# New matmul durations in a planner: fp32r matmuls of 256 and 512 columns

## The chip, the cores and the metric

The kernel runs on one core of a Trainium2 chip, as one launch. The metric is the device time in microseconds (us), the median of several executions. A core has a matmul engine (TensorE; PE in the profile, PEld for its weight loads), three engines for elementwise work (VectorE is DVE, ScalarE is ACT, GpSimd is POOL) and a queue engine (SyncE, SP), which here issues most loads; POOL issues the loads that add to what is already in the buffer.

## The reference

Two layers over 512 rows of width 1024, all in fp32. Each layer is a feed-forward part, a token mixing part and a second feed-forward part, and an RMS norm closes the whole:

```python
for l in range(DEPTH):                                   # DEPTH = 2
    x = x + 0.5 * swiglu_ffn(rmsnorm(x, ffn1_norm[l]), ffn1_w_in[l], ffn1_w_out[l])
    h = rmsnorm(x, mix_norm[l])
    u_rwkv, u_gla, u_xa, u_gate = split_cols(h @ w_in[l], ...)
    y_rwkv, v_first = rwkv7_mixer(u_rwkv, v_first, ...)
    y_gla = gla_mixer(u_gla, ...)
    y_xa = memory_attention(u_xa, rmsnorm(mem, mem_norm[l]), xa_w_kv[l])
    branches = jnp.stack([y_rwkv, y_gla, y_xa], axis=2)
    gates = jax.nn.sigmoid(u_gate.reshape(b, s, N_BRANCH, d))
    x = x + jnp.einsum('bsjc,jcd,bsjd->bsd', branches, w_branch[l], gates) @ w_out[l]
    x = x + 0.5 * swiglu_ffn(rmsnorm(x, ffn2_norm[l]), ffn2_w_in[l], ffn2_w_out[l])
return rmsnorm(x, final_norm)

def swiglu_ffn(h, w_in, w_out):                          # w_in 1024 x 5632, w_out 2816 x 1024
    gate, up = jnp.split(h @ w_in, 2, axis=-1)
    return (jax.nn.silu(gate) * up) @ w_out
```

## The kernel before

**Matmuls.** Activations lie transposed in SBUF: 128 partitions of a width tile by 512 rows, and a half of the rows is 256 columns. A large product in near fp32 is made of fp32r matmuls: each operand is split into a high part (a copy in fp32r, made on ACT: `hi`, `hl`, `mh`, `whi`) and a low part (source minus high part, made on DVE: `lo`, `hl` again where one tile holds both, `ml`, `wlo`), and three matmuls give high by high, high by low and low by high. In the mixing part such products have 512 columns, beside many small matmuls, most of them in fp32. In the feed-forward parts nearly all are 256 columns wide.

**Feed-forward parts.** They run as a chain of jobs (`seven`, L931). A job is one 2 x 2 block product of weights and activations, done with seven half products in place of eight, from sums and differences of the blocks. Its weights come as `wraw`, `q`, `e` (named `q` in the profile) and `d`; the loads on POOL add a block to one that SP has loaded. DVE makes two more sums of weights, `q<-wraw` and `q<-q`, and ACT and DVE split each weight. The half products gather in three PSUM tiles: X is `ps_b`, Y is `ps_i`, Z is `ps_f` and `ps_c` in turn. ACT copies X into Y once, early in the job: the row `ps_i<-ps_b`. In the first phase of a block (from `w_in`) the evictions give `ft` and `fm`, and then `mh`, `ml` and `s` (operands for the second phase); in the second phase (from `w_out`, the down products) each PSUM tile is added to the residual on DVE: `x<-ps_i`, `x<-ps_c`, `x<-ps_f`, `x<-ps_b`. `chain` (L982) starts a job before the former is ended, so the next job's weight sums stand among the former's evictions.

**What sets the order.** Nothing is issued when the network's functions run. A `Recorder` notes every operation with its dependencies, and `cost` (L353) gives each a `busy` (how long it keeps its engine) and a `took` (until its result is there). `plan` then simulates the five engines. `run` takes on PE the ready matmul that is first in the program, small ones ahead of large products, and in the current mode if it can (`choose`); on the other engines it takes the ready operation with the smallest due time. Due times come from `urgency`: PE's order of the last simulation is added up by `busy`, and from there the time goes back through `took`. This is done six times, each with due times from the order before it, and the order with the earliest simulated end is kept. `issue` emits it, so that each engine's queue holds its instructions in this order. Hence all instructions have the line L318 in the profile, the line that emits.

Of the kernel before, what the change touches and what calls it, by code (L numbers as in the profile page):

```python
# [286 lines left out]
class Recorder:  # L287
# [65 lines left out]
    def cost(self, o, ins, outs, a, k):  # L353

        out = outs[0] if outs else None
        col = any(v.n == 1 and not v.flat for v in ins[1:])
        psum = any(v.psum for v in ins)
        if o.engine == "tensor":
            n = out.n
            wide = ins[0].n > 64  # L360
            if o.what == "transpose":
                o.busy, o.took = 109, 275
            elif ins[0].dt == F32R:
                o.busy = n / 2.4 + 13.7
                o.took = n / 2.4 + 177
            else:
                o.busy = 2 * max(108 if wide else 58, 2 * n / 2.4 + 2.7)
                if self.tiles > 1:
                    o.busy = 2 * max(108 if wide and n <= 64 else 54, 2 * n / 2.4 + 2.7)
                o.took = o.busy / 2 + 2 * n / 2.4 + 168  # L370
                o.busy = max(o.busy / self.tiles, 110 if wide else 56)
            up = lambda q: 32 if q <= 32 else 64 if q <= 64 else 128
            o.mode = (o.what != "transpose" and ins[0].dt == F32R, up(ins[0].rows[1] - ins[0].rows[0]), up(ins[0].n))
        elif o.engine == "vector":
            n = max(v.n for v in ins + outs)
            if o.what == "reciprocal":
                o.took = 130 + 6.3 * n
            elif o.what == "tensor_tensor_scan":
                o.took = 139 + 2.11 * n
            elif o.what == "memset":  # L380
                o.took = 60 + n / 0.96
            else:
                fast = o.what in ("tensor_scalar", "tensor_copy") and not psum
                o.took = ((n / 2 if fast else n) + 151) / 0.96 + (55 if col and o.what != "tensor_tensor" else 0)
            o.busy = max(o.took - 80, 60)
        elif o.engine == "scalar" and o.what != "dma_start":
            n = out.n
            o.took = 0.83 * n + (166 if psum else 207) + (90 if col else 0) + (95 if "accum_out" in k else 0)
            o.busy = o.took - 90 + (100 if "accum_out" in k else 0)
            o.table = {AF.Tanh: "exp", AF.Exp: "exp", AF.Sqrt: "sqrt", AF.Ln: "ln", AF.Silu: "silu",  # L390
                       AF.Sigmoid: "sig"}.get(a[2])
        elif o.engine == "gpsimd" and o.what == "dma_start":
            o.pipe = 4 * out.n * P / 190
            o.busy, o.took = 1000, o.pipe + 2950
        elif o.engine == "gpsimd":
            o.took = 95 + 0.84 * out.n
            o.busy = o.took
        else:
            some = ins + outs
            size = 4 * some[0].n * (1 if some[0].flat else some[0].rows[1] - some[0].rows[0])  # L400
            o.pipe = size / 230
            o.busy, o.took = 440 if o.engine == "scalar" else max(440, o.pipe), o.pipe + 1450
# [1539 lines left out]
```

## Time and profile before

| | |
|---|---|
| median of 3 executions | 2520.64 us (2519.31 to 2521.92) |
| the profiled execution | 2520.57 us, its span 2518.8 us |
| mean granted TensorE clock | 0.998 of full speed |
| instructions in the span | 47196, of them 17636 on PE |
| large stretches | first layer: FFN 1 to about 340 us, mixing to 885, FFN 2 to 1252; second layer: FFN 1 to 1585, mixing to 2130, FFN 2 and the closing norm to the end |

The profile is of one execution. Busy shares are those of the span; an engine's rows can overlap, since the next instruction starts before the last is through, so the step from one start to the next tells what an instruction costs in a row of them. In timeline rows stand the start, the duration, engine, line, operation, the tiles (out<-in), the shape and a count, and in brackets the engine's idle time ahead of it with what ended it.

### The profile page before, as it was taken

Reading aid. Unit: us, or ns where it says so; the run is one execution under the profiler, and the core shown is the slowest. Engines: PE = TensorE matmul, PEld = TensorE weight load, DVE = VectorE, ACT = ScalarE, POOL = GpSimd, SP = SyncE. Lnnn points to the kernel's source line nnn. Section 1 sums busy time; section 2 is a strip of 40 time slices with the busy share of each in tenths; the row PEclk is TensorE's granted clock in tenths of the full one; section 3 lists DMA queues with packets and bytes.
Section 4 is the critical chain, followed back from the end, with each engine's and each line's share of the span. In section 5 each row is a group of like instructions: output and inputs, shape, how many; then the busy total and the mean of one; then the engine's idle time right before and its main releaser. Section 6 shows DMA issues by size and latency. Waiting matters only on the chain.

```text
span 2518.8 us, 47196 instructions
## 1 busy us (share of the span) xinstructions
PE 2490.5 (99%) x17636; PEld 2241.0 (89%) x17636; DVE 2096.8 (83%) x4218; ACT 1468.8 (58%) x2660; POOL 241.3 (10%) x363
## 2 busy tenths in 40 slices
PE   9999999999999999999999999999999999999998
PEld 8999988888788899999989999877887888899998
DVE  8988886688888689988899889766879877898888
ACT  6665666564554456565665656674645434565655
POOL 1121100000000001211111111000000000011110
PEclk9999999999999999999999999999999999999999
DMA  7787762322222456877658787523322225468774
GB/s 196 200 203 191 173 188 74 117 75 70 75 77 74 144 159 152 209 192 185 158 138 190 190 189 185 162 90 93 90 67 84 68 78 172 134 164 197 190 185 107
DMA packets 163669, 358.02 MB, mean 142 GB/s; under 512 B 18257, under 2 KB 38161, under 8 KB 163441
## 3 DMA queue, kind: packets, MB, share of 16 engines
q1 hardware_dynamic: 125344, 288.87, 36.8%
q0 software_dynamic: 36864, 65.03, 16.6%
q8 instruction: 139, 2.28, 0.4%
q10 hardware_dynamic: 1232, 1.11, 0.1%
q14 instruction: 90, 0.73, 0.1%
HBM read 342.88 MB, written 12.06 MB: 141 GB/s over the span
## 4 chain that ended last, share of the span: by engine, by line
PE 85%; DVE 8%; DMA 3%; ACT 2%; issue 2%; POOL 0%; DVEq 0%; SPq 0%; ACTq 0%; POOLq 0%
PE ps_b L318 43%; PE ps_i L318 24%; PE ps_f L318 9%; PE ps_c L318 8%; PE ps_y L318 2%; DMA q<-in_ffn_out_dram 1%; DVE lo L318 1%; DVE hl L318 1%; DVE wlo L318 1%; DMA wraw<-in_ffn_in_dram 1%; DVE x L318 1%; DVE ml L318 1%; DMA wraw<-in_ffn_out_dram 0%; DVE q L318 0%; ACT whi L318 0%
## 5 line engine op out<-in xcount | busy, mean ns | idle before, releaser
L318 PE MATMUL ps_b<-xhi,whi 128*128 128x512 f32 (+1 forms) x880 | 356.4, 405 | 0.2 <-DVE rk_r L318 0.2
L318 PE MATMUL ps_b<-xlo,whi 128*128 128x512 f32 (+1 forms) x880 | 355.9, 405 | 0.1
L318 PE MATMUL ps_b<-xhi,wlo 128*128 128x512 f32 x864 | 349.8, 405 | 0.3 <-DVE wlo L318 0.3
L318 DVE TENSOR_TENSOR wlo<-wraw,whi 128x1024 fp32r<-128x1024 f32 (+1 forms) x172 | 183.7, 1068 | 78.8 <-ACT whi L318 76.3
L318 ACT ACTIVATE whi<-wraw 128x1024 fp32r<-128x1024 f32 (+1 forms) x174 | 161.8, 930 | 135.8 <-PE ps_b L318 104.0
L318 ACT ACTIVATE hl<-q 128x512 fp32r<-128x512 f32 (+1 forms) x256 | 158.0, 617 | 117.5 <-PE ps_f L318 28.3
L318 ACT ACTIVATE hi<-wraw 128x1024 fp32r<-128x1024 f32 (+2 forms) x162 | 166.5, 1028 | 100.4 <-PE ps_i L318 42.7
L318 DVE TENSOR_TENSOR lo<-wraw,hi 128x1024 fp32r<-128x1024 f32 (+2 forms) x162 | 191.2, 1181 | 26.3 <-ACT hi L318 25.2
L318 PEld LDWEIGHTS ps_b<-xlo,whi 128*128 128x128 f32 (+1 forms) x880 | 164.5, 187 | 37.6 <-DVE xlo L318 2.4
L318 PEld LDWEIGHTS ps_b<-xhi,whi 128*128 128x128 f32 (+1 forms) x880 | 164.8, 187 | 35.9 <-issue 1.2
L318 PEld LDWEIGHTS ps_b<-xhi,wlo 128*128 128x128 f32 x864 | 163.1, 189 | 33.6 <-DVE wlo L318 0.9
L318 DVE TENSOR_TENSOR hl<-q,hl 128x512 fp32r<-128x512 f32 (+1 forms) x256 | 170.3, 666 | 8.8 <-ACT hl L318 8.0
L318 ACT ACTIVATE hi<-q 128x1024 fp32r<-128x1024 f32 (+1 forms) x128 | 131.9, 1031 | 70.2 <-PE ps_b L318 46.3
L318 DVE TENSOR_TENSOR lo<-q,hi 128x1024 fp32r<-128x1024 f32 (+1 forms) x128 | 151.8, 1186 | 17.5 <-ACT hi L318 17.0
L318 PE MATMUL ps_i<-mh,hl 128*128 128x256 f32 x832 | 140.7, 281 | 0.9 <-DVE x L318 0.7
L318 PE MATMUL ps_b<-xhi,hi 128*128 128x256 f32 x576 | 139.8, 279 | 0.0
L318 PE MATMUL ps_b<-xlo,hi 128*128 128x256 f32 x576 | 139.3, 278 | 0.0
L318 DVE TENSOR_TENSOR q<-q 128x512 f32<-128x512 f32 (+1 forms) x128 | 85.5, 668 | 53.8 <-DMA q<-in_ffn_in_dram 40.0
L318 PEld LDWEIGHTS ps_i<-mh,hl 128*128 128x128 f32 x832 | 120.7, 190 | 1.6 <-ACT hl L318 0.9
L318 ACT ACTIVATE hl<-d 128x512 fp32r<-128x512 f32 (+1 forms) x128 | 78.9, 617 | 63.4 <-PE ps_i L318 44.3
L318 PE MATMUL ps_i<-t,hl 128*128 128x256 f32 x864 | 115.2, 283 | 0.0
L318 PE MATMUL ps_i<-xhi,hl 128*128 128x256 f32 x576 | 109.7, 276 | 0.0
(430 smaller groups left out, 7165.1 us busy)
## 6 DMA issues: line engine op xcount, KB each, us to landing
wraw<-in_w_main_dram SPq DMA_DIRECT2D x108, 512.0 KB, 3.7
wraw<-in_ffn_in_dram SPq DMA_DIRECT2D x102, 512.0 KB, 4.9
q<-in_ffn_in_dram SPq DMA_DIRECT2D x144, 256.0 KB, 4.1
d<-in_ffn_in_dram SPq DMA_DIRECT2D x72, 256.0 KB, 4.3
q<-in_ffn_in_dram POOLq DMA_DIRECT2D x72, 256.0 KB, 6.2
wraw<-in_ffn_in_dram POOLq DMA_DIRECT2D x72, 256.0 KB, 4.9
wraw<-in_ffn_out_dram SPq DMA_DIRECT2D x32, 512.0 KB, 5.2
q<-in_ffn_out_dram SPq DMA_DIRECT2D x64, 256.0 KB, 3.6
```

The source lines that it names most:

```text
L318: return getattr(getattr(self.tc.nc, engine), what)(*(f(v) for v in a), **{n: f(v) for n, v in k.items()})
```

## The change

One line in `cost` gives the planner another `busy` for every fp32r matmul; `n` is the number of columns:

```diff
             elif ins[0].dt == F32R:
-                o.busy = n / 2.4 + 13.7
+                o.busy = 0.4512 * n - 1.3
                 o.took = n / 2.4 + 177
```

For 256 columns the planner now counts 114.2 ns instead of 120.4, for 512 columns 229.7 instead of 227.0. The delay until the result can be used, `took`, is the same. No operation is added, removed or altered. The instructions themselves are the same, 16344 matmuls among them, of which 10708 are fp32r with 256 columns and 4064 with 512. The planner keeps the second of its six orders before, and the sixth now. Against before, 4335 matmuls stand at another place in PE's queue (by 1.8 places on average over all, 81 at most), 2548 of 4218 instructions on DVE, 992 of 2562 on ACT, 101 of 864 on SP (by three places at most) and 13 of 359 on POOL. PE's queue changes from fp32r to small fp32 matmuls and back 326 times before, 333 times now.

DVE, in the down products of the last feed-forward part, at about 2286 to 2295 us in the profile before. `q<-wraw` and `q<-q` are the weight sums, `lo` and `hl` low parts, `x` the evictions. Before:

```order
L318 SCALAR_TENSOR_TENSOR x<-ps_b,x 128x256
L318 TENSOR_TENSOR q<-q 128x512
L318 TENSOR_TENSOR q<-wraw 128x512
L318 SCALAR_TENSOR_TENSOR x<-ps_f,x 128x256
L318 TENSOR_TENSOR lo<-wraw,hi 128x1024
L318 TENSOR_TENSOR q<-q 128x512
L318 TENSOR_TENSOR hl<-q,hl 128x512
L318 SCALAR_TENSOR_TENSOR x<-ps_i,x 128x256
L318 SCALAR_TENSOR_TENSOR x<-ps_c,x 128x256
L318 TENSOR_TENSOR hl<-q,hl 128x512
L318 SCALAR_TENSOR_TENSOR x<-ps_i,x 128x256
```

and now:

```order
L318 SCALAR_TENSOR_TENSOR x<-ps_f,x 128x256
L318 TENSOR_TENSOR lo<-wraw,hi 128x1024
L318 SCALAR_TENSOR_TENSOR x<-ps_b,x 128x256
L318 TENSOR_TENSOR hl<-q,hl 128x512
L318 SCALAR_TENSOR_TENSOR x<-ps_i,x 128x256
L318 TENSOR_TENSOR q<-q 128x512
L318 TENSOR_TENSOR hl<-q,hl 128x512
L318 SCALAR_TENSOR_TENSOR x<-ps_i,x 128x256
L318 TENSOR_TENSOR q<-wraw 128x512
L318 SCALAR_TENSOR_TENSOR x<-ps_c,x 128x256
```

The next job's `q<-wraw` moved from ahead of `x<-ps_f` to behind the second `x<-ps_i`, and `q<-q` to between the two `x<-ps_i`; the second `q<-q` of before, of a job later, is behind the part shown. The same sums change places with the evictions at about 1370 us, and `q<-wraw` with one `x<-ps_i` at about 1159 us.

ACT, at the start of a block's second phase in the first feed-forward part of the second layer, at about 1336 to 1340 us. `hl` is the high part of a weight, `mh` that of an operand, `ps_i<-ps_b` the copy of X into Y. Before:

```order
L318 ACTIVATE mh<-s_15561 128x256
L318 ACTIVATE hl<-d 128x512
L318 ACTIVATE hl<-q 128x512
L318 ACTIVATE mh<-s_15580 128x256
L318 ACTIVATE fm<-ps_f 128x256
L318 ACTIVATE ps_i<-ps_b 128x256
L318 ACTIVATE hi<-wraw 128x1024
```

and now:

```order
L318 ACTIVATE hl<-d 128x512
L318 ACTIVATE mh<-s_15575 128x256
L318 ACTIVATE ps_i<-ps_b 128x256
L318 ACTIVATE hl<-q 128x512
L318 ACTIVATE mh<-s_15595 128x256
L318 ACTIVATE fm<-ps_f 128x256
L318 ACTIVATE hi<-wraw 128x1024
```

`ps_i<-ps_b` moved from behind `fm<-ps_f` to ahead of `hl<-q`, past three instructions. The same move is found at about 92, 1007 and 2256 us.

## The prediction

> **What bounds the kernel now.** I read the page first: the busy times and the chain that ended last.
>
> ```profile
> PE 2490.5 (99%) x17636; PEld 2241.0 (89%) x17636; DVE 2096.8 (83%) x4218; ACT 1468.8 (58%) x2660; POOL 241.3 (10%) x363
> PE 85%; DVE 8%; DMA 3%; ACT 2%; issue 2%; POOL 0%; DVEq 0%; SPq 0%; ACTq 0%; POOLq 0%
> ```
>
> PE, the matmul engine, is busy for 2490.5 of 2518.8 us and carries 85% of the chain. The change issues the same instructions with the same operands, so those 2490.5 us stay (their spacing apart), and only the 28.3 us outside them can move. Next I cut the span by stage: FFN 1, mixing and FFN 2 of the first layer, then of the second (columns: stretch, its us, then the busy time and count of PE, PEld, DVE, ACT and POOL, the granted clock, DMA share, GB/s).
>
> ```profile
> 0.00:340.00 340.00, 335.71 (x2682) 324.27 (x2683) 302.47 (x558) 217.50 (x389) 53.53 (x71) 1.00 0.76 194
> 340.00:885.00 545.00, 541.66 (x3183) 441.90 (x3182) 416.23 (x960) 293.88 (x554) 13.03 (x50) 1.00 0.31 95
> ...
> 1585.00:2130.00 545.00, 542.54 (x3157) 437.55 (x3156) 420.03 (x967) 298.10 (x557) 12.99 (x56) 1.00 0.32 96
> 2130.00:2518.80 388.80, 375.78 (x3019) 364.55 (x3017) 336.77 (x610) 228.81 (x403) 55.03 (x64) 0.98 0.66 165
> ```
>
> The two mixing stages leave PE idle for 545.00 − 541.66 = 3.3 us and 2.5 us, 5.8 in all. The last stage has 13.0 us, its closing norm and stores included, and the only clock under 1.00. Then PE's waits, grouped by what they waited for (total us, times, longest):
>
> ```profile
> PE ps_i L318 <- DVE x L318: 4.5, 4, 2.3
> PE ps_b L318 <- DVE xrl L318: 1.4, 2, 0.7
> ...
> PE ps_c L318 <- ACT mh L318: 0.8, 1, 0.8
> ```
>
> The largest group is the `x` eviction on DVE: a down product may not go on in PSUM `ps_i` before DVE has added its former contents to `x`. So the question is not matmul speed, but which of these short waits a new order takes away, and which it makes.
>
> **Term 1, DVE's sums move behind the evictions.** At the longest wait:
>
> ```profile
> 2290.79 0.62 PE L318 MATMUL ps_i<-mh,lo 128*128 128x256 f32 x4
> ...
> 2295.04 0.91 PE L318 MATMUL ps_i<-ml,hl 128*128 128x256 f32 x4 [2.28 <-DVE x L318]
> ```
>
> PE would have gone on at 2295.04 − 2.28 = 2292.76. DVE's rows say why it could not:
>
> ```profile
> 2286.96 0.67 DVE L318 TENSOR_TENSOR q<-q 128x512 f32<-128x512 f32 x1
> 2289.94 0.69 DVE L318 TENSOR_TENSOR q<-wraw 128x512 f32<-128x512 f32 x1 [2.31 <-DMA wraw<-in_ffn_in_dram]
> 2290.55 0.42 DVE L318 SCALAR_TENSOR_TENSOR x<-ps_f,x 128x256 f32<-128x256 f32 x1
> 2290.88 1.22 DVE L318 TENSOR_TENSOR lo<-wraw,hi 128x1024 fp32r<-128x1024 f32 x1
> 2292.01 0.69 DVE L318 TENSOR_TENSOR q<-q 128x512 f32<-128x512 f32 x1
> ...
> 2294.48 0.41 DVE L318 SCALAR_TENSOR_TENSOR x<-ps_i,x 128x256 f32<-128x256 f32 x1
> ```
>
> `q<-wraw`, a sum of weights for the next job, stood idle for 2.31 us for its load, with the evictions queued behind it. At 1370 us it is the same, and the wait on PE follows:
>
> ```profile
> 1370.86 0.69 DVE L318 TENSOR_TENSOR q<-wraw 128x512 f32<-128x512 f32 x1 [1.52 <-DMA wraw<-in_ffn_in_dram]
> ...
> 1376.05 0.71 PE L318 MATMUL ps_i<-ml,hl 128*128 128x256 f32 x4 [1.55 <-DVE x L318]
> ```
>
> After the change this `q<-wraw` stands directly behind that `x<-ps_i` (first pair of order rows). What DVE then has between `q<-q`'s place and the eviction is eight instructions: four `x` additions, one of them the eviction itself, at 0.33 (the step from 2290.55 to 2290.88), a `lo` at 1.13, and three 512-wide ones at about 0.61, together 4.3 us. DVE is through at 2286.96 + 4.3 = 2291.3 if the PSUM is ready; the product evicted ends at 2290.79 + 0.62 = 2291.41, so the eviction runs until about 2291.85, 0.9 us before PE needs it. The load had landed by 2289.94, so the moved sum itself no longer waits. At 1376 and at a third place, 1160 us, the order changes in the same way. I take the whole group: −4.5 us. Ends: −4.5, and 0 if the waits form again.
>
> The moved sum ends some 2 us later. Its reader is the next job's weight split on ACT,
>
> ```profile
> 2306.27 1.06 ACT L318 ACTIVATE hi<-q 128x1024 fp32r<-128x1024 f32 x1 [0.56 <-PE ps_b L318]
> ```
>
> 14 us further on and waiting for PE: covered.
>
> **Term 2, the clock.** Behind the 2.28 us wait, but not behind the 1.55 us one:
>
> ```profile
> 2295.40:2298.70 3.30, 3.30 (x18) 3.30 (x17) 1.96 (x4) 0.63 (x1) 0.86 (x1) 0.50 0.91 247
> 1376.00:1380.00 4.00, 3.95 (x34) 3.98 (x35) 2.99 (x5) 1.00 (x2) 0.79 (x1) 1.00 0.95 262
> ```
>
> For 3.3 us the granted clock was 0.50, with 18 matmuls instead of about 30: half of 3.3, 1.65 us, lost. If the wait goes, I take −1.65; ends −1.65 and 0. The Trainium skill, "TensorE: Matmul & The Clock Gate", section "What's actually happening", has the clock fall after at least one idle window of about 3.4 us. Here a 2.28 us wait sufficed, while the length at half clock does agree; by the page's threshold this wait could not have caused the drop, term 2 would be 0 and the sum 1.65 higher.
>
> **Term 3, an eviction moves ahead on ACT.** At about 1338 us (second pair of order rows), and likewise at 92, 1007 and 2256 us, `ps_i<-ps_b` moves ahead of `hl<-q`, `mh` and `fm`. Before:
>
> ```profile
> 1336.57 0.62 ACT L318 ACTIVATE hl<-d 128x512 fp32r<-128x512 f32 x1
> 1337.27 0.63 ACT L318 ACTIVATE hl<-q 128x512 fp32r<-128x512 f32 x1
> 1337.81 0.40 ACT L318 ACTIVATE mh<-s 128x256 fp32r<-128x256 f32 x1
> 1338.11 0.36 ACT L318 ACTIVATE fm<-ps_f 128x256 f32<-128x256 f32 x1
> 1338.38 0.38 ACT L318 ACTIVATE ps_i<-ps_b 128x256 f32<-128x256 f32 x1
> ...
> 1337.06 0.62 PE L318 MATMUL ps_b<-mh,lo 128*128 128x256 f32 x4
> 1338.26 0.38 PE L318 MATMUL ps_c<-mh,hi 128*128 128x256 f32 x1
> 1338.53 0.38 PE L318 MATMUL ps_f<-xhi,hl 128*128 128x256 f32 x1
> ```
>
> `mh` ends at 1338.21 and PE reads it at 1338.26: no slack. In the new order ACT must first wait for `ps_b`, which ends at 1337.68. `ps_i` then starts at 1337.70, `hl` 0.30 later, `mh` 0.54 after that: 1338.54, ending at 1338.94, and PE goes on at about 1339.00, 0.74 late. `fm` ends at 1339.20, just in time again. Three places make 2.2; at 92 us PE already waits 0.8 for `mh` (the row above), and I add the eviction's 0.3 to the full 0.74, middle 0.5. Together +2.7. Ends: 0, if PE comes later there anyway, and 4 × 0.74 = +3.0.
>
> **Term 4, changes of mode.** PE pays when a small fp32 matmul stands between fp32r ones:
>
> ```profile
> 591.43 0.40 PE L318 MATMUL ps_b<-xlo,whi 128*128 128x512 f32 x1
> 591.67 0.38 PE L318 MATMUL ps_y<-S,AR 128*128 128x128 f32 x2
> 591.80 0.48 PE L318 MATMUL ps_b<-xhi,wlo 128*128 128x512 f32 x1
> 592.12 0.39 PE L318 MATMUL ps_b<-xhi,whi 128*128 128x512 f32 x1
> ```
>
> The fp32r matmul after it takes 0.32 until the next start instead of 0.24. The new order has 333 such changes, the old 326: 7 × 0.08 = +0.6; ends 0 and +1.
>
> **Term 5, everything else.** In the mixing stages the order is redrawn on all engines: as many producers lose slack as gain it, so I take 0; ends −5.8 (all its idle time) and +5.8 (twice it). Near 1015, 1348 and 2266 us PE takes the first `ps_b` matmuls of a job 0.6 us earlier, against 0.3 us of slack on ACT's `hi<-wraw`, but that split also moves ahead, of `hl<-q`: 0, at most 3 × 0.3 = +0.9. SP's and POOL's loads shift by three places at most; the 14 us above are more than such a step: 0.
>
> **The sum:** −4.5 − 1.65 + 2.7 + 0.6 = −2.85. The profiled execution took 2520.57 us (span 2518.8 and 1.8 around it), 0.07 under the median of the three runs, 2520.64. So 2520.57 − 2.85 = 2517.7. A measurement here tells some 0.2%, 5 us, from no change: "the same".
>
> **The rivals.**
>
> *Faster.* ACT's swap costs nothing, because PE arrives at `mh` 0.7 us later in its own new order: −4.5 − 1.65 + 0.6 = −5.55, 2515.0. Half of the mixing stages' idle time gone would lead to about the same place (−2.85 − 2.9). For it: a planner with matmul durations nearer to the trace (the steps of the 256-wide rows here are 0.11 to 0.12) should put producers where they are needed. Against: PE's rows around 1338 keep their order.
>
> *The waits form again.* The loads still land late, and other evictions behind the moved sums hold PE up equally long: −2.85 + 4.5 + 1.65 = +3.3, 2523.9. For it: this DVE is 83% busy. Against: 0.9 us to spare.
>
> *The half clock isn't the wait's.* If the drop at 2295 us has another cause and recurs, as the threshold in the skill's page would have it, term 2 is 0: 2520.57 − 1.2 = 2519.4. Against: it is the only drop in the row of that stage, and follows its longest wait.
>
> *Slower.* The sum now stands ahead of the evictions `x<-ps_c` and `x<-ps_b`. If the load that it needs lands later than DVE reaches it, about 2291.8, those two wait, and PE at `ps_c` with them, now long enough for the half clock at each of the three places: 3 × (2.28 + 1.65) = 11.8 on top of −2.85, +8.95, 2529.5. It decides from a landing about 2 us later than 2289.9, and beats 0.2% when each place costs over (5.0 + 2.85) / 3 = 2.6 us. Against: the load's issue stays in its place on POOL's queue. A lesser form is one such wait of 3.9 us in each mixing stage, both layers being planned alike: −2.85 + 7.8 = +5.0, 2525.6.
>
> **How the numbers follow.** The forecast 0.30; faster 0.33; waits again 0.10; clock 0.08; slower 0.19, half of it mixing. So faster than 0.2% 0.33, within it 0.48, slower 0.19. The range: down to terms 1, 2 and half of the mixing stages' idle time, 2520.57 − 6.15 − 2.9 = 2511.5; up past the second rival, and to the lesser form of the slower one, with the +0.9: 2526.5.
>
> **What would show it.** In the waits, the group `ps_i <- DVE x` shrinks below 1 us and `ps_c <- ACT mh` grows to 3; `q<-wraw` no longer carries an idle time ahead of an eviction; the last stage's clock is 1.00; PE's busy time falls by less than 2 us. I am wrong if the mixing stages' idle time differs by more than 3 us, or if a wait over 2 us stands anywhere else.

## The result and the profile after

The changed kernel takes 2508.77 us, the median of five executions (2507.01 to 2512.15), against 2520.11 us (2518.33 to 2521.92) for the kernel before on the same chip: a ratio of 0.9957, 95% interval 0.9942 to 0.9971, so 11.3 us or 0.43% faster. The prediction's 2517.7 us and its range from 2511.5 missed this; it stood for "the same". On the other chips of this study the kernel before took 2515.4 to 2516.7 us; a second set of executions of the changed kernel on one of them took 2508.56 us, 0.9969 (0.9959 to 0.9979), 8.1 us faster.

One statement on the change has to be set right: the planner keeps the sixth of its orders before and the second now, not the other way round. No term of the sum rests on it.

The profiled execution took 2507.01 us, its span 2504.9 us. First the page, busy times and the chain:

```profile
PE 2478.0 (99%) x17636; PEld 2231.3 (89%) x17636; DVE 2097.1 (84%) x4218; ACT 1468.5 (59%) x2660; POOL 241.4 (10%) x363
PE 87%; DVE 7%; DMA 2%; ACT 1%; issue 1%; DVEq 0%; ACTq 0%; SPq 0%; POOLq 0%
```

The span fell by 13.9 us, and **PE's busy time by 12.5 of them**, from 2490.5 to 2478.0, with the same 17636 matmuls. What lies outside PE's busy time went from 28.3 to 26.9 us. The stretches, with the columns as before (the last row is the place of the half clock):

```profile
0.00:340.00 340.00, 335.13 (x2699) 324.40 (x2700) 303.56 (x560) 219.50 (x391) 53.52 (x71) 1.00 0.77 194
340.00:885.00 545.00, 541.37 (x3176) 440.92 (x3175) 417.14 (x962) 294.58 (x554) 13.17 (x50) 1.00 0.33 95
...
1585.00:2130.00 545.00, 540.32 (x3117) 433.87 (x3116) 416.10 (x964) 293.42 (x554) 13.01 (x50) 1.00 0.32 95
2130.00:2504.90 374.90, 364.68 (x2974) 354.92 (x2972) 331.21 (x600) 224.88 (x397) 54.38 (x63) 0.98 0.68 168
2290.00:2310.00 20.00, 20.00 (x178) 20.00 (x177) 15.22 (x26) 12.27 (x23) 3.45 (x4) 1.00 0.88 217
```

In the first stretch PE issues 2699 matmuls where it issued 2682, though it is busy for 0.6 us less: it does more in the same busy time. In PE's waits (total us, times, longest) the two groups that the prediction spoke of changed as it said, `x` from 4.5 to 0.5 and `mh` from 0.8 to 3.1:

```profile
PE ps_c L318 <- ACT mh L318: 3.1, 4, 1.3
PE ps_f L318 <- DVE qs L318: 1.8, 2, 1.0
PE ps_b L318 <- DVE xrl L318: 1.4, 2, 0.7
PE ps_f L318 <- DVE y L318: 1.3, 4, 0.5
PE ps_i L318 <- ACT hl L318: 1.2, 1, 1.2
...
PE ps_i L318 <- DVE x L318: 0.5, 1, 0.5
```

All recorded waits together went from 17.6 us (67 waits) to 17.2 (52): what went at some places came back at others. So the sum of the waits that the profile names makes up nothing of the gain.

### Where busy time can shrink

A 256-wide fp32r matmul is recorded as 0.28 us long (the profile models the end of a matmul), but the next one starts 0.113 us later. While one is in flight PE counts as busy, even if the next is held up; the profile shows no idle time, only a longer step between two starts. So I summed the steps from start to start (time above 113.3 ns, us) over all pairs of such matmuls, and the same in the second profiles of both programs (`again`, `after_again` below):

| part of PE's time | before | after | before, second profile | after, second profile |
|---|---|---|---|---|
| steps over 126 ns, their recorded idle time taken off | 17.3 (186) | 6.6 (58) | 15.4 (171) | 7.7 (67) |
| steps under 126 ns: slower pace | 14.2 | 10.1 | 14.9 | 12.2 |
| recorded waits | 17.6 | 17.2 | 12.8 | 17.6 |
| other steps (512 columns, small fp32) | 1232.6 | 1235.0 | 1233.2 | 1235.3 |

Before to after: −10.7 (2.0 of it the half clock's matmuls) −4.1 −0.4 +2.4 = −12.8 of the span's −13.9; the rest lies at the ends and with matmuls whose records are missing. Between the second profiles the span fell by only 4.4 us (2512.9 to 2508.5): −7.7 −2.7 +4.8 +2.1 = −3.5, since the recorded waits grew by 4.8 there, a wait of 2.46 us for ACT's `hl` among them, which the first profile after has as 1.22. The long steps and the pace shrank in both pairs; the waits shrank by 0.4 us in the first and grew in the second. By stages, the long steps fell from 14.6 to 4.1 us in the four feed-forward parts, and from 2.8 to 2.6 in the two mixing parts.

What stands at the long steps is the eviction of `ps_i`, at dozens of jobs. A half product into `ps_i` is evicted, and the next half product but one goes on in the same PSUM tile. One such place before, PE and then DVE:

```profile
227.75 0.62 PE L318 MATMUL ps_b<-mh,lo 128*128 128x256 f32 x4
228.26 0.71 PE L318 MATMUL ps_i<-ml,hl 128*128 128x256 f32 x4
...
226.37 0.68 DVE L318 TENSOR_TENSOR hl<-q,hl 128x512 fp32r<-128x512 f32 x1
227.09 0.69 DVE L318 TENSOR_TENSOR q<-wraw 128x512 f32<-128x512 f32 x1
227.70 0.42 DVE L318 SCALAR_TENSOR_TENSOR x<-ps_i,x 128x256 f32<-128x256 f32 x1
```

and after:

```profile
227.51 0.62 PE L318 MATMUL ps_b<-mh,lo 128*128 128x256 f32 x4
227.96 0.62 PE L318 MATMUL ps_i<-ml,hl 128*128 128x256 f32 x4
...
226.46 0.69 DVE L318 TENSOR_TENSOR hl<-q,hl 128x512 fp32r<-128x512 f32 x1
227.06 0.42 DVE L318 SCALAR_TENSOR_TENSOR x<-ps_i,x 128x256 f32<-128x256 f32 x1
227.39 0.69 DVE L318 TENSOR_TENSOR q<-wraw 128x512 f32<-128x512 f32 x1
```

Before, the weight sum `q<-wraw` stands ahead of the eviction, which ends at 228.12 instead of 227.48. The matmuls that need it start 0.51 us behind the group ahead instead of 0.45, and their group of four takes 0.71 instead of 0.62: 0.15 us lost, and no bracket. I call an eviction **late** if it ends less than 200 ns before the start of the matmul that needs it. Of some 190 such evictions (`x<-ps_i` on DVE, `ft<-ps_i` on ACT) 55 were late before and cost 12.35 us, recorded waits included; after, 2 cost 0.78. Those that end 200 to 300 ns ahead cost nothing (19 in the profile after).

Of the 12.35 us, 5.3 are recorded idle time; without it the late evictions fell from 7.0 us to 0.3, and in the second profiles from 7.0 to 0.6. That is 6.7 of the 10.7 us by which the long steps fell, and 6.4 of 7.7. The half clock is another 2.0 of the 10.7; what made the other long steps was not followed up.

In all 55 the evicting engine was busy right up to the eviction. But only 19 have the weight sum `q<-wraw` directly ahead of them: 12 stand behind a low part `hl<-q,hl`, 12 are evictions on ACT, all behind an `mh` or `hl`, and the other 12 behind various work on DVE.

### The profile page after: what moved, and what is told of

Read it like the earlier page. It is cut to its first block, busy times and chain, and to the rows that moved or that the text cites. A ratio compares the mean times of both kernels' runs of the same rounds, so it can differ in the third digit from the quotient of the medians.

```text
span 2504.9 us, 47243 instructions
## 1 busy us (share of the span) xinstructions
PE 2478.0 (99%) x17636; PEld 2231.3 (89%) x17636; DVE 2097.1 (84%) x4218; ACT 1468.5 (59%) x2660; POOL 241.4 (10%) x363
## 3 DMA queue, kind: packets, MB, share of 16 engines
q8 instruction: 139, 2.28, 0.4%
## 4 chain that ended last, share of the span: by engine, by line
PE 87%; DVE 7%; DMA 2%; ACT 1%; issue 1%; DVEq 0%; ACTq 0%; SPq 0%; POOLq 0%
PE ps_b L318 42%; PE ps_i L318 25%; PE ps_f L318 10%; PE ps_c L318 9%; PE ps_y L318 1%; DVE wlo L318 1%; DMA q<-in_ffn_out_dram 1%; DVE ml L318 1%; DVE lo L318 1%; DMA wraw<-in_ffn_out_dram 0%; DVE x L318 0%; DMA wraw<-in_w_out_dram 0%; DVE xn L318 0%; DMA yd<-sg 0%; ACT whi L318 0%
## 5 line engine op out<-in xcount | busy, mean ns | idle before, releaser
L318 PEld LDWEIGHTS ps_b<-xhi,hi 128*128 128x128 f32 x576 | 108.5, 188 | 0.2
```

The source lines that it names most:

```text
L318: return getattr(getattr(self.tc.nc, engine), what)(*(f(v) for v in a), **{n: f(v) for n, v in k.items()})
```

## The experiments

Letters in the quoted expectations: L is the theory that late evictions carry the gain, P that the pace of matmuls does (by where operands lie in SBUF), D that evictions are late because the planner leaves them too small a margin, R that they are late because it holds PE for slower, against DVE and ACT, than it is. Ratios are against the kernel before, on the same chip. Microseconds "above the changed kernel" are against its 2508.56 us in `after_again`, which ran on one chip with `later_a`, `slack145_b` and `slack0_a`; for the other runs they compare two chips, on which the kernel before differed by up to 1.3 us.

### Is the loss fixed by the program?

`again` is the kernel before, unchanged.

> The kernel before, unchanged, profiled a second time. Theory L (late evictions: in the order of before, weight sums on DVE stand ahead of the evictions that PE needs next, and PE is held up by some 0.1 us at many jobs, which the profile counts as busy because the former matmul is still in flight) and theory P (pace: the matmuls run slower where the SBUF addresses of their two operands stand badly to each other) both hold that this is fixed by the program: PE's busy time again 2490 us within 1.5, and the same 180 or so stretched steps between matmuls. Rival C (chance: which matmuls run slowly differs from execution to execution): PE's busy time moves by several us, at other places.

2514.82 us. PE busy 2489.8; 171 long steps and 52 late evictions (9.14 us). These come again, so the loss is in the program and not in one execution. But one group changed from 4.5 us:

```profile
PE ps_i L318 <- DVE x L318: 0.9, 2, 0.6
```

So most of the recorded `x` wait, the 2.28 us one with the half clock among it, belonged to the first execution, in which a load landed late ahead of a sum on DVE.

### Which number carries it?

`n256`, the 256-wide duration alone:

```diff
-                o.busy = 0.4512 * n - 1.3
+                o.busy = 0.4512 * n - 1.3 if n <= 256 else n / 2.4 + 13.7
```

> The change for up to 256 columns alone; 512 columns keep the old duration. The order differs from that of after in about a fifth of PE's places, but few weight sums stand directly ahead of x<-ps_i evictions (14, as in after; 29 before), and the SBUF places are those of after. Theories L and P: all of the gain, 2508 to 2512. Rival: the gain is a lucky order, and any redrawn order is as likely to lose: anywhere between 2505 and 2530. If the 512-column duration made the gain: 2520.

2507.79 us, 0.9965 (0.9952 to 0.9978); 4 late evictions, 0.89 us. The whole gain, as expected. The 512-wide number does nothing that can be measured.

### The sums moved by hand

`behind8`: the planner's old order, and then each weight sum on DVE that stands at most eight places ahead of an `x<-ps_i` is put directly behind it, where its users allow:

```diff
-        return order
+        return self.moved(order)
```

> The order of before with one thing changed: each weight sum on DVE that stands up to eight places ahead of an x<-ps_i eviction goes directly behind it. Nothing else moves, the SBUF places stay. Theory L: the recorded waits of ps_i for x (4.5 us), the stretched steps behind late x evictions (about 3 us) and the half clock (2 us) go: 6 to 9 us faster than before, about 2512. Theory P: no placement changes, at most 1 us. What the prediction had as its terms 1 and 2 alone: 6 us faster, with PE's busy time down by 2.

2523.38 us, 1.0030 (1.0017 to 1.0044): slower, a miss. Late evictions fell only to 33 (11.15 us), PE's busy time stayed at 2491.0, and other waits appeared or grew:

```profile
PE ps_i L318 <- DVE x L318: 3.7, 9, 0.8
PE ps_b L318 <- ACT mh L318: 2.6, 4, 1.1
PE ps_c L318 <- DVE x L318: 1.7, 1, 1.7
```

DVE is busy for 83% of the span, and what one instruction gains by a move, those that it passes may lose; which of them made these waits was not followed up. This neither confirms L nor refutes it. `ahead_a` turns it round: the changed kernel, with each sum that stands up to two places behind an `x<-ps_i` put ahead of it, where its sources allow (61 evictions then have one directly ahead, 14 in the changed kernel):

```diff
-        return order
+        return self.ahead(order)
```

> The order of after with one thing changed: a weight sum on DVE that stands up to two places behind an x<-ps_i eviction goes directly ahead of it (61 such, 14 in after). Theory L in the form that is left (an eviction that ends under 200 ns before its matmul costs 70 to 110 ns more than the profile's waits show): 30 or more late evictions, 3 to 7 us slower than after. Rival: what counts is the rest of the order, and the sums' places cost nothing by themselves: within 1.5 us of after.

2513.09 us, 0.9990 (0.9980 to 1.0000), 4.5 us above the 2508.56 of the changed kernel; 23 late evictions (6.82 us); PE busy 2484.1 against 2481.5. Time as expected, fewer late evictions than expected. Nothing else is edited here, so this shows that weight sums ahead of evictions cost time: 0.26 us at each of the 20 places that became late (6.82 − 1.67 us; 15 of the 23 late evictions have `q<-wraw` directly ahead, 5 `q<-q`). It also shows that most sums there do no harm: 41 of the 61 evictions with one directly ahead are not late.

### Why are they late: margin or rates?

The planner has a margin, `SLACK` (60 ns), by which it wants results early. `slack145_b` raises it in the kernel before; `slack0_a` takes 85 ns off in the changed one, what the twelve matmuls of a half product were over-counted by (12 × 7.0 = 84, 120.4 against the trace's 113.4):

```diff
-    HOP, SLACK = 34, 60
+    HOP, SLACK = 34, 145      # slack145_b; slack0_a has -25
```

> The kernel before with its old matmul durations; only the planner's margin between a producer's end and the matmul that needs it (SLACK) is 145 ns instead of 60. Theory D (due times): before counts 120.4 ns for a 256-column matmul that takes 113.4, so an eviction that is planned just in time behind twelve matmuls ends 12 x 7 = 84 ns too late; 55 of 192 evictions of ps_i end under 200 ns before the matmul that waits for them in the trace of before, at 70 to 110 ns and more each, 3 of 193 in that of after. The wider margin gives the 84 ns back: under 10 such evictions, 6 to 9 us faster than before. The tile of the mixing part's end stays at its slow place, so the pace costs 1 us more than in after. Theory P (pace by placement): no gain. Rival luck: any redrawn order lands anywhere within 10 us of before, and the count of late evictions does not tell where.

2518.50 us, 1.0003 (0.9994 to 1.0012), 48 late (9.28 us).

> The kernel after with its new durations; the margin SLACK is cut from 60 to -25 ns, by the 84 ns that the new durations gave. Theory D: evictions end late again, 40 or more of 192 under 200 ns before their matmul, and most of the gain is lost: 5 to 9 us slower than after, near before. Theory P: the SBUF places stay as in after, so within 2 us of after. Luck: no relation.

2512.63 us, 0.9985 (0.9976 to 0.9995), 3 late (0.68 us); the 4 us above the changed kernel are from elsewhere. Both miss, and D falls: 85 ns more or less of margin hardly changes how many evictions are late.

Then the rates. `slower_b` is the kernel before with all DVE and ACT durations 6% longer in the planner, so that PE's stand to them as in the changed kernel; `faster_a` is the changed kernel with them 5.7% shorter, as before the change:

```diff
+        if engine in ("vector", "scalar") and what != "dma_start":
+            o.busy, o.took = 1.06 * o.busy, 1.06 * o.took      # faster_a: 0.943
```

> Before with its old matmul durations (120.4 ns for 256 columns, 6% over the 113.4 of the trace) and the planner's durations of all DVE and ACT instructions raised by 6% as well, so that the engines' rates to each other are right again; absolute times and the margin are no better. Theory R (rates): with PE counted too slow the planner sees holes on DVE ahead of an eviction that is not ready yet, and puts a weight sum of 0.6 us into them; on the chip the product ends earlier, the hole isn't there, and the eviction is late. In this order 18 of 156 such evictions have a sum directly ahead of them, against 29 before and 14 after. Under R: at most 15 of some 190 evictions end under 200 ns before their matmul (52 to 55 in before), and it is 5 to 8 us faster than before, less the 1 us for the slow tile that stays. If absolute durations count: as before.

10 late (4.23 us), as R says, but 2526.37 us, 1.0047 (1.0031 to 1.0064), where less was expected. The evictions of `ps_c` had become late instead:

```profile
PE ps_c L318 <- DVE x L318: 5.0, 3, 2.6
PE ps_b L318 <- ACT hi L318: 3.1, 5, 0.7
```

Two stretches of 3.4 us at half clock, at 1010 and 1344 us, took some 3.4 us more in the profiled execution.

> The reverse: after with its new matmul durations, and DVE's and ACT's planner durations cut by 6%. The matmul durations are right, the rates are as wrong as before. 38 of 156 evictions have a weight sum directly ahead. Theory R: 40 or more late evictions, 6 to 9 us slower than after (2508.6 on the chip of the batch before), near or over before. If right matmul durations are what counts: as after.

66 late (16.05 us), as R says, and 2544.73 us, 1.0122 (1.0104 to 1.0140), 36 us above the changed kernel and more than expected.

`p117` and `p110` give 256 columns 117 and 110 ns instead of 114.2 (in the kernel before, with the new 512):

```diff
-                o.busy = n / 2.4 + 13.7
+                o.busy = 117 if n == 256 else 0.4512 * n - 1.3     # p110: 110
```

> Half the step: 117 ns for 256 columns, 512 columns as in after. 35 sums stand directly ahead of an eviction. Theory R by that count: 35 or more late evictions, within 3 us of before, although the SBUF places are those of after. If the gain grew evenly with the duration: 4 us faster than before. Luck: anything.

13 late (1.57 us), 2510.30 us, 0.9984 (0.9973 to 0.9996): half the step already brings most of the gain, and far fewer are late than I expected.

> Beyond the step: 110 ns for 256 columns, 3% under the trace. 15 sums stand directly ahead of an eviction. Theory R: under 15 late evictions; the planner now takes PE for too fast and will be late elsewhere, but not at these: 4 to 9 us faster than before. If only the right value helps: as before or slower.

3 late (1.92 us), but 2514.79 us, 1.0002 (0.9993 to 1.0011), no gain. Too fast a PE in the plan has its price too; the high parts on ACT are late now:

```profile
PE ps_b L318 <- ACT hi L318: 2.7, 4, 0.7
PE ps_b L318 <- ACT whi L318: 2.5, 4, 0.8
```

By duration, then: 120.4 ns gives 52 to 55 late, 117 gives 13, 114.2 gives 2 to 4, 110 gives 3; and of these four the time is least at 114.2. R foretold the count in three of the four runs made for it (`slower_b`, `faster_a`, `p110`). In `p117` it missed, 13 for 35 or more: the count had been foretold from the sums directly ahead of an eviction, and these don't tell it (before 29 and 55 late, `p117` 35 and 13). Over all these plans the count falls as PE's durations fall against those of DVE and ACT, down to a floor of 2 to 4. The time follows the count only where nothing else becomes late; R's forecast of the time held in `faster_a` alone, in direction.

### The pace

Steps between 113 and 126 ns have two causes that could be told apart. In the kernel before, `hl`, the weights of the product that ends the second layer's mixing, lay elsewhere than after: tiles are placed in the order in which they are first made, and this follows the plan. There, 2137 to 2170 us, the steps were 118 ns. `place_b` shifts the first layer's tile of the same kind by 64 bytes:

```diff
-            lead, rest = (SHIFT, REST) if pool.name == "mg" else (0, 0)
+            lead, rest = ((SHIFT, REST) if self.l == 0 else (0, SHIFT + REST)) if pool.name == "mg" else (0, 0)
```

> The order of before; only the weight tile hl of the output product that ends the second layer's mixing part starts 64 bytes lower, so that its distance to the moving operand is 192 (mod 256) as everywhere else, and no longer 128. It concerns 144 matmuls and some 120 between them, which run at 118 ns instead of 113.5 in the trace of before. Theory P: about 1.2 us faster, with steps of 113 to 114 ns between 2137 and 2170 us. If pace is the main part of the change: 4 us or more. Theory L alone: 0.

2515.04 us, 0.9992 (0.9979 to 1.0005): too small to measure (the steps under 126 ns sum to 13.6 us above base against 14.9 in `again`). `base_a` does it on a large scale: in the changed kernel the tile `vm` is begun 64 bytes lower, and with it some 5400 matmuls have weights and moving operand a multiple of 256 bytes apart, instead of 192 more than one.

```diff
-              for t, o in (("vm", SHIFT), ("kT", 0))]
+              for t, o in (("vm", 0), ("kT", 0))]
```

> The order and durations of after; the tile vm is 64 bytes shorter, so that the tiles behind it (x and y operands) all stand 64 bytes lower and their distance to the weights is 0 (mod 256) instead of 192, for some 5400 matmuls of the w_in jobs. Theory P: 4.5 to 5.5 ns more for each: 22 to 30 us slower than after, near 2535, with no more recorded waits. Rival (order, not place): within 2 us of after.

2531.85 us, 1.0064 (1.0048 to 1.0080), 23 us above the changed kernel, as expected, with 2 or 3 late evictions and hardly other waits. The same 30 us of the plan, after and in `base_a`:

```profile
60.00:90.00 30.00, 30.00 (x264) 30.00 (x263) 29.75 (x57) 22.60 (x45) 5.17 (x6) 1.00 0.76 185
```

```profile
60.00:90.00 30.00, 30.00 (x253) 30.00 (x252) 28.89 (x55) 21.29 (x43) 4.91 (x6) 1.00 0.76 185
```

PE is busy for all 30.00 us at clock 1.00 in both; 264 matmuls against 253. The step is 113.4 ns at distance 192 and 120.0 ns at distance 0. That the sum came out near the expectation is partly luck. The slower pace of the 256-wide steps adds 33 us in the profile of `base_a` (45.2 us above base against 12.5 in `after_again`), but the same 64 bytes bring some 2600 of the 512-wide fp32r matmuls from 192 to 0 as well, and these become faster: 229.4 ns on average at distance 0 in `base_a` against 233.1 at 192 in the profile after. All steps that aren't 256 wide take 9.8 us less. The distance that is good for 256 columns is thus the worse one for 512. P is a real cause, but a small one in this change: the steps at other distances than 192 sum to 6.8 us above base before and to 6.2 after.

Most of the slow steps stand at distance 192, however: some 1350 matmuls with steps of 116 to 121 ns before, 1440 in `again`, 570 after, 1100 in `after_again`. There PE has two rhythms, 113.4 and 117.8 ns, and stays in one for long runs. I thought the 896 `t3` matmuls at distance 0, twelve or eight to a job, brought on the slow one, and moved them to 192 (`t3_a`; `t3_later` adds the edit of `later_a` below):

```diff
-            return self.c * H if self.low else (12 + self.c) * H + SHIFT
+            return self.c * H + REST if self.low else (12 + self.c) * H
```

> The order and durations of after; only SBUF places change: the operand t3 of each job's third half product (in vm for the w_in jobs, in the m tiles for the w_out jobs) is moved by 64 or 192 bytes, so that for 896 matmuls the distance between moving operand and weights is 192 (mod 256) as for the 9400 others, and no longer 0. Theory P (pace goes by that distance: 113.4 ns at 192, 118 to 119.5 at 0 or 128, and the slow pace goes on for two or three matmuls behind): these take 113 to 114 ns, 4 to 6 us faster than after (2508.6). Rival: the third product is slow because it takes all low parts before the high ones and changes weights at each matmul: 0.

2520.03 us, 1.0013 (1.0001 to 1.0025): 11 us slower where 4 to 6 faster were expected. The moved matmuls went from 118.8 to 116.1 ns on average, all others from 113.9 to 115.3. Where after had

```profile
212.00:252.00 40.00, 40.00 (x353) 40.00 (x353) 34.06 (x62) 20.51 (x32) 7.76 (x9) 1.00 0.79 191
```

`t3_a` had

```profile
212.00:252.00 40.00, 40.00 (x342) 40.00 (x342) 34.30 (x63) 19.36 (x29) 6.90 (x8) 1.00 0.77 187
```

with up to 423 matmuls on end in the slow rhythm (50 at most in the profile after, but 178 and 260 in two stretches of `after_again`, which have no matmul at distance 0 in them).

> The moved t3 operands together with ps_i<-ps_b back behind fm on ACT: the version that should beat both. By theory P 4 to 6 us for the place, and by the batch before 0.6 for ACT: 2502 to 2504. If place does nothing: 2508.

2519.05 us, 1.0014 (1.0003 to 1.0025), the same again. The stretch at distance 0 seems to end the slow rhythm, not to begin it. `all_a` leaves no such stretch (`vm` and `kT` changed places as well):

```diff
-              for t, o in (("vm", SHIFT), ("kT", 0))]
+              for t, o in (("vm", 0), ("kT", SHIFT))]
```

> The order and durations of after; now no 256-column matmul of the feed-forward parts is left at distance 0: t3 stands at 192 in kT as well. In t3_a four matmuls per job (kT) stayed at 0; they put PE into steps of 117.8 ns, and it stayed in them for up to 423 matmuls at distance 192. Theory G (two rhythms at distance 192, 113.4 and 117.8 ns; matmuls at distance 0 and late operands bring PE into the slow one; a run of some eight or more at distance 0 ends in the fast one): with no kT left to start it, slow stretches begin only at late operands. If those are rare starters, 4 to 8 us faster than after, 2501 to 2505. If a late operand is enough and nothing brings the fast rhythm back, slower than after, 2512 to 2525, with slow stretches of over 100 matmuls that begin at waits.

2516.37 us, 1.0001 (0.9987 to 1.0016), 8 us slower than the changed kernel, and its executions lie 16 us apart (2506.05 to 2521.88). In the profiled one ten stretches in the slow rhythm hold some 2630 matmuls, the longest 781; the long ones begin behind 512-wide matmuls or right behind a long step, with recorded idle time or without. Four of them begin at places where the profile after has a slow stretch too: there it ends after 48 matmuls, here after 329. So an interruption can bring PE into the slow rhythm, and it can stay there for hundreds of matmuls. But the profiled execution was a fast one (2507.71 us), and its slow pace sums to 12.8 us, as in `after_again` (12.5); that the pace made the other executions slower is not shown. What makes the two rhythms is open.

### The new wait for `mh`

`later_a`: the changed kernel with the four `ps_i<-ps_b` of term 3 back behind `fm`.

```diff
-        return order
+        return self.later(order)
```

> The order of after; at the four places where ps_i<-ps_b moved ahead of hl, mh and fm on ACT it goes back behind fm. The prediction's term 3: PE's wait of ps_c for mh, 3.1 us in the trace of after and 0.8 in that of before, goes back to about 1, and the kernel is 2 to 2.5 us faster than after. Rival: the wait only moves to ps_i, which then comes later: 0.

2507.96 us, 0.9973 (0.9964 to 0.9983), against 2508.56 for the changed kernel again, `after_again`:

> The kernel after, unchanged, on the chip of this batch, to be compared with the three others and with before. Theory D: 7 to 12 us faster than before on the same chip, and again at most 5 evictions of ps_i under 200 ns ahead of their matmul.

```profile
PE ps_c L318 <- ACT mh L318: 2.2, 4, 1.0
```

Only 0.9 of the 3.1 us went, and 0.6 us of the time, less than these runs can tell. ACT's queue and PE at the place of 1333 us in the profile after say why:

```profile
1334.51 0.63 ACT L318 ACTIVATE hl<-q 128x512 fp32r<-128x512 f32 x1 [0.60 <-PE ps_b L318]
...
1335.50 0.39 PE L318 MATMUL ps_c<-mh,hi 128*128 128x256 f32 x1 [0.40 <-ACT mh L318]
```

With the eviction out of the way `hl<-q` itself waits 0.60 us for PE's `ps_b`, and `mh` stands behind it: 0.40 of the 0.62 us remain. No version was measurably faster than the changed kernel; `n256` (0.9965) and `later_a` (0.9973) lie within its interval.

## Why the prediction was wrong

**The step that failed** is the premise "those 2490.5 us stay (their spacing apart), and only the 28.3 us outside them can move". It names the spacing of the matmuls and then gives it no term in the sum. 12.5 us of the 13.9 came out of PE's busy time, by steps that became shorter: 6.7 us at late evictions, 4.1 by the pace, 2.0 at the half clock and 2.0 at other long steps, less 2.4 that the other steps grew by. Its sign "PE's busy time falls by less than 2 us" was wrong by a factor of six, and the range's lower end, made of idle time and the half clock (which lies in busy time, against the premise), could not hold the result. The waits view, which I used as the list of all that an order could change, names a hold-up only when PE runs empty.

**Term 1** had the right mechanism in the right rows and the wrong number of places. At the three places all went as described; the eviction of 2294.48 is now ahead of the sum, with no bracket behind it:

```profile
2283.70 0.69 DVE L318 TENSOR_TENSOR hl<-q,hl 128x512 fp32r<-128x512 f32 x1
2284.30 0.42 DVE L318 SCALAR_TENSOR_TENSOR x<-ps_i,x 128x256 f32<-128x256 f32 x1
2284.64 0.69 DVE L318 TENSOR_TENSOR q<-wraw 128x512 f32<-128x512 f32 x1
2285.24 0.42 DVE L318 SCALAR_TENSOR_TENSOR x<-ps_c,x 128x256 f32<-128x256 f32 x1
```

The group fell by 4.0 of the 4.5 us taken. But `again` shows that 3.6 of these were that one execution's; what the program itself loses is at 52 to 55 evictions, most of them without a recorded wait: 45 in the first profile, which cost 0.10 us each on average. For late evictions the term should have been −11.6 (12.35 to 0.78), or −7.5 by the second pair of profiles (9.14 to 1.67); of the recorded idle time in it, 4.9 us, as much came back at other places. The cause lies in the number that was changed: with 120.4 ns the planner ends a half product of 12 matmuls 84 ns too late against 113.4, seven of them 0.59 us. It thus sees room ahead of an eviction for one more piece of work, such as a weight sum on DVE with its step of 0.60 us, and on the chip there is none. That the count of late evictions goes with the ratio of PE's durations to those of DVE and ACT is shown (`n256`, `slower_b`, `faster_a`, `p117`). That each passes through just such a hole is argued: it was read in the rows at 227 us, only 19 of the 55 have the weight sum directly ahead, and no run tested them one by one.

**Term 2**: the clock is 1.00 at 2290 to 2310 us, and the 18 matmuls gave back 2.0 us where 1.65 was taken; but `again` has no such stretch, so this too was that one execution's. The sign "the last stage's clock is 1.00" was badly chosen: the stage still shows 0.98, from its end, where the clock is 0.50 for the last 12 us and PE has little left to do. Which wait brings the half clock is less plain than the term had it. In `p117` a wait of 2.84 us, up to 123.91 us, is followed by half clock (the second row; the first is the 3.4 us ahead of it):

```profile
121.46:124.88 3.42, 0.97 (x8) 0.97 (x9) 0.99 (x2) 0.90 (x2) 0.86 (x1) 1.00 0.99 293
124.88:128.29 3.41, 3.41 (x19) 3.41 (x18) 2.61 (x6) 2.18 (x3) 0.86 (x1) 0.50 0.85 178
```

and in `slower_b` one of 2.60 us, up to 2305.51 us, is not:

```profile
2303.65:2307.07 3.42, 1.56 (x13) 1.56 (x14) 2.40 (x5) 0.33 (x1) 0.00 (x0) 1.00 0.80 181
2305.50:2308.80 3.30, 3.29 (x28) 3.29 (x29) 1.94 (x3) 1.98 (x4) 0.66 (x1) 1.00 0.48 159
```

So 2.28 us had sufficed before and 2.60 did not; in `slack0_a` 1.86 us sufficed, and in `slower_b` two groups of waits of 0.5 and 0.7 us did. The length of the wait alone does not decide. The clock records of the traces show what else does: within each of the 19 executions every change of the clock lies on a grid of 3.413 us (in `slower_b` the two drops are 334.51 us apart, 98 such steps). The rows from 121.46, 124.88 and 2303.65 us are periods of that grid. Among the periods that hold nothing but 256-wide matmuls, some 6700 in all traces, a full one has 30 starts; all four with 8 to 12 starts were followed by half clock (before, `p117`, `slack0_a`, `slower_b`), one of four with 13, and none with 14 or more. The wait of 2.60 us lies across two periods, and the emptier of them has 13. So what counts seems to be how little PE does within one period; this is read from the records, and no run was made to test it. The rule of the Trainium skill ("TensorE: Matmul & The Clock Gate", "What's actually happening"), an idle window of about 3.4 us, would have none of these drop if idle means wholly idle; the drops speak against it as it stands.

**Term 3** was right in place and nearly in size, 0.8 to 3.1 us where +2.7 was taken, but only in part in its mechanism. ACT and then PE at the place that was worked out in advance:

```profile
1332.30 0.37 ACT L318 ACTIVATE ps_i<-ps_b 128x256 f32<-128x256 f32 x1 [0.55 <-PE ps_b L318]
1332.58 0.62 ACT L318 ACTIVATE hl<-q 128x512 fp32r<-128x512 f32 x1
1333.10 0.41 ACT L318 ACTIVATE mh<-s 128x256 fp32r<-128x256 f32 x1
1333.40 0.38 ACT L318 ACTIVATE fm<-ps_f 128x256 f32<-128x256 f32 x1
...
1332.66 0.28 PE L318 MATMUL ps_c<-ml,hi 128*128 128x256 f32 x1
1333.56 0.38 PE L318 MATMUL ps_c<-mh,hi 128*128 128x256 f32 x1 [0.62 <-ACT mh L318]
```

`ps_i`, `hl` and `mh` follow at 0.28 and 0.52 (0.30 and 0.54 were taken), `mh` ends at 1333.51, and PE waits 0.62 (0.74 was taken). But `later_a` shows that the eviction's move makes only 0.2 of the 0.62: ACT waits for PE's `ps_b` at that point of the new order even without it. **Term 4**, +0.6 for seven mode changes, is within the +2.4 of the other steps and was not separated. **Term 5** was taken as 0: between the same matmuls of the plan, the recorded waits of the two mixing parts went from 6.5 to 8.3 us, +1.8 and inside its bound of 3; the feed-forward parts made up for it. But the busy time had a term of its own that nobody named, the pace, −4.1 us here and −2.7 between the second profiles; of that, the tile at 2137 us is explained (0.6 us), and the rest is the slow rhythm at distance 192, which differs by 2.2 us between the two profiles of the changed kernel and is thus partly chance.

Of the rivals, "faster" named the right direction and even the right ground (a planner with truer matmul durations puts producers where they are needed), but priced it in idle time: 2515.0. It had 0.33, a little more than the forecast's own 0.30, so the prediction leaned to the right side without the right path. What it set against this rival was that PE's rows around 1338 keep their order; they did not have to change, since DVE's did. The slower rival did not come: no wait over 1.3 us stands in the profile after, and the longest in `after_again` is the 2.46 us for `hl`, which no term named.

## What to carry to other kernels

When PE is 99% busy, look at steps from start to start, not at busy time: a hold-up shorter than a matmul's time in flight (here 0.28 us against a step of 0.113) is counted as busy and named by no wait, and dozens of them can come to as much as all recorded waits (here 17.3 us of long steps against 17.6 of waits). In a planner the durations of the engines matter as ratios: here a PE that was 6% too slow let other work in ahead of evictions, which a wider margin did not mend, and one that was 3% too fast made other producers late. Take a recorded wait for a property of the program only if a second profile has it too.

## What the runs showed of the hardware

- The step of 256-wide fp32r matmuls depends on the distance of the two operands' addresses in SBUF: 113.4 ns where it is 192 modulo 256 bytes, 118 to 120 where it is 0 or 128 (`base_a`: 120 throughout). For 512-wide ones it is the other way: 233.1 ns on average at 192 (after), 229.4 at 0 (`base_a`).
- At distance 192 there are two rhythms of the 256-wide steps, 113.4 and 117.8 ns, and the slow one can last for hundreds of matmuls (up to 781 in `all_a`, 260 in `after_again`). With the 8 to 12 matmuls at distance 0 moved away from each job, it lasted longer at the same places (329 matmuls in `all_a` against 48 after), and `t3_a` took 11 us more; a cause is not shown.
- A PSUM tile that came free 50 to 200 ns before the recorded start of the matmul that needs it cost 0.10 us on average without idle time in the profile (45 evictions before); 200 to 300 ns cost nothing.
- The clock changed only on a grid of 3.413 us within each execution, and half clock between matmuls lasted one such step. Among the periods of the grid with 256-wide matmuls alone it followed those in which PE had started 8 to 12 of them in place of 30 (before, `p117`, `slack0_a`, `slower_b`) and one of four with 13, but none with 14 or more.
